# Order of the four weight sums, and the place of one quarter's parts, in the seven-product pairs of an output projection

## The chip, the core and the metric

The program runs on one core of one Trainium2 chip. The core has five engines with queues of their own that run at the same time and wait for each other through semaphores: TensorE (matmuls; PE in the profile, with its weight loads as PEld), VectorE (DVE), ScalarE (ACT), GpSimd (POOL) and SyncE (SP, which here only starts transfers). The metric is the device time of one execution in microseconds. Smaller is better.

## What is computed

Two layers of a decoder trunk, for 256 tokens of width 2048, all in float32. What matters of one layer:

```python
proj = rmsnorm(x) @ w_in[l]                       # 2048 -> 6144
q, k, v, gate_b, gate_c, conv_in = split(proj)    # 1024 columns each
attn = diff_attention(q, k, v)                    # 8 heads
conv = gate_b * short_conv(gate_c * conv_in)
x = x + concatenate([attn, conv]) @ w_out[l]      # the out-projection, 2048 -> 2048
x = x + relu(rmsnorm(x) @ w_up[l])**2 @ w_down[l] # 2048 -> 8192 -> 2048
```

## The kernel before

**Parts.** Each float32 operand of a matmul is held as two float32r tiles: hi, the rounded value (a ScalarE copy), and lo, the rest (a VectorE subtraction of hi from the value). A product is three matmuls: hi x hi, hi x lo, lo x hi. A weight thus comes as a load into a raw tile (started by SP), a copy on ScalarE and a subtraction on VectorE, and then TensorE can use it. A "split" or "rounding" below is this pair; the VectorE half is the last of it.

**Stages.** In each layer: q, k, v and the convolution's inputs; then the out-projection, whose left half (output columns 0 to 1023, `BySeven.left`, L939) is interleaved with the eight columns of the gate B projection; then its right half (`BySeven.right`, L1012); then the MLP.

**Sevens.** The out-projection goes over eight pairs i of 256 rows of w_out. Over a half of the output columns a pair is a 2 x 2 product of blocks. A "seven" makes it with seven products in place of eight (the scheme of Strassen and Winograd), for which sums of the blocks are needed: of the activations S1 to S4 (`sums_of`, L805), of the weights four sums in a tile t (`sums`, L854). With b11, b21 the left blocks and b12, b22 the right blocks of the weights, t[0] = b12 - b11, t[1] = b22 - b12, t[2] = t[1] + b11, t[3] = b21 - t[2]. The left half has five sevens (pairs 0 to 4, called a0 to a4 here for their first part and b0 to b4 for the second) and the right half two (pairs 2 and 3); the other pairs go the ordinary way, as chunks such as (0,5), which is output chunk 0 of pair 5. Two layers make fourteen sevens.

**The jobs of one seven** (`jobs`, L824), in the order in which they are taken:

- `plain` loads the left and the right raw tile (L842), splits b11 and b21 into the room w7b (pool tag "b"), and splits b22 into a tile whi and a tile wlo of wpool. All splits of this class have the lines L829 (ScalarE) and L830 (VectorE).
- `sums` forms t[0] (L859) and t[1] (L860), splits both into the room w7x, and forms t[2] (L864) and t[3] (L865).
- `more` splits t[2] and t[3] into the room w7y. w7x and w7y are the two buffers of biasp.

TensorE uses them in `product` (L881, matmuls at L884): first b11, b21, b22 (with S4) and t[0]; after another gate column t[1], then t[2] and t[3].

**Gate columns.** `column` (L948) makes one gate column out of two jobs with 128 columns of w_in each (splits at L326 and L327 by `halves`, L320; matmuls at L417), into one PSUM bank that all columns but the first share. `gate` (L771) then evicts the bank by ScalarE (L774), and VectorE forms y (L775, L776) and its parts (cat, L778 and L779). The next column can begin when the bank has been evicted. `LEFT` (L39) is the order, written out by hand: columns 0 and 1, a0, column 2, b0, column 3, a1, column 4, b1, column 5, a2, column 6, b2, column 7, a3, b3, the chunks (0,5) and (1,5), a4, b4, and the last chunks.

**Buffers.** All raw tiles of the stage share four buffers (`RAW`), so a load waits until the last reader of a raw tile is done. Each tile hi and each tile lo of the ordinary weights comes from wpool, with three buffers of each, also b22's. Jobs are made three ahead of their use (`take`, L381; `AHEAD`). The buffer "ao" of the pool tmp is a single one, 128 partitions by two times 512 float32; attention uses it (L650), and so does `results` (L905), which joins the seven products at the end of a half.

**What sets the order.** Only TensorE's instructions keep the order of the program text (`manual_schedule`), and single instructions that are marked `late`. Those of the other engines are ordered when the program is built, by a schedule on estimated times (`schedule_with_timeline_sim=True`). Each engine then works through its list in that order and waits at the first instruction that isn't ready.

Of the kernel before, what the change touches and what calls it, by code (L numbers as in the profile page):

```python
# [10 lines left out]
F32R = mybir.dt.float32r  # L11
# [4 lines left out]
P = 128  # L16
# [12 lines left out]
CH = 512  # L29
# [97 lines left out]
def trunk(ctx: ExitStack, tc: tile.TileContext, x, w_in, w_out, conv_w, q_norm_g, k_norm_g,  # L127
          lambda_q1, lambda_k1, lambda_q2, lambda_k2, subln_g, attn_norm_g, mlp_norm_g,
          w_up, w_down, rel_bias, selector, out):
    nc = tc.nc  # L130
# [4 lines left out]
    wpool = ctx.enter_context(tc.tile_pool(name="wpool", bufs=3))  # L135
# [650 lines left out]
    class BySeven:  # L786
# [37 lines left out]
        def jobs(self, w, i, col):  # L824

            mine = {}

            def split(hi, lo, src):
                nc.scalar.activation(hi, src, AF.Copy)  # L829
                nc.vector.tensor_sub(lo, src, hi.bitcast(F32))  # L830
                return hi, lo

            def two(room, src):

                hi, lo = split(room[:, 0], room[:, 1], src)
                return [(hi[:, j], lo[:, j]) for j in range(2)]

            def plain():
                raws = []
                for n in range(2):  # L840
                    raw = self.weights.pool.tile([P, 2, CH], F32, tag="raw", name="raw", bufs=RAW)
                    nc.sync.dma_start(  # L842
                        raw, w[2 * P * i:2 * P * (i + 1),
                               col + n * CH:col + (n + 1) * CH].rearrange(
                            "(k p) c -> p k c", p=P))
                    raws.append(raw)
                mine["raw"] = raws
                room = self.pool.tile([P, 2, 2, CH], F32R, tag="b", name="w7b")
                b11, b21 = two(room, raws[0])
                hi = wpool.tile([P, 2, CH], F32R, tag="hi", name="whi")  # L850
                lo = wpool.tile([P, 2, CH], F32R, tag="lo", name="wlo")
                return b11, b21, split(hi[:, 0], lo[:, 0], raws[1][:, 1])

            def sums():  # L854
                left, right = mine["raw"]
                pool, tag = (self.pool, "b") if col else (self.kpool, "kL")
                t = mine["t"] = pool.tile([P, 4, CH], F32, tag=tag, name="w7t")

                nc.vector.tensor_sub(t[:, 0], right[:, 0], left[:, 0])  # L859
                nc.vector.tensor_sub(t[:, 1], right[:, 1], right[:, 0])  # L860
                room = self.biasp.tile([P, 2, 2, CH], F32R, tag="bias", name="w7x")
                made = two(room, t[:, 0:2])

                nc.vector.tensor_add(t[:, 2], t[:, 1], left[:, 0])  # L864
                nc.vector.tensor_sub(t[:, 3], left[:, 1], t[:, 2])  # L865
                return made

            def more():
                room = self.biasp.tile([P, 2, 2, CH], F32R, tag="bias", name="w7y")
                return two(room, mine["t"][:, 2:4])  # L870

            return [plain, sums, more]

        def form(self, i, pa, a):
# [734 lines left out]
```

## Time and profile before

| what | us |
|---|---|
| median of three runs | 2130.81 |
| lowest and highest of them | 2129.49, 2132.07 |
| the profiled execution, its own time | 2129.56 |
| its span, from the first to the last instruction | 2127.8 |
| the left half of the out-projection in the first layer (from some 265 to 344 us), the gate columns ahead of it from 254 us | about 90 |
| the same in the second layer (from some 1323 to 1402 us), the gate columns from 1312 us | about 90 |

A row of a timeline reads: start, duration, engine, line, operation, tile written <- tiles read, partitions x elements and type, how many in a row. In square brackets stands how long the engine was idle before it and what ended that. A row of the waits reads: engine, its tile and line, <- the engine, tile and line it waited for: microseconds in all, times, the longest. A window's row reads: the stretch, its length, and then the busy time of TensorE, of its weight loads, of VectorE, of ScalarE and of GpSimd, each with its number of instructions, the granted clock of TensorE, the busy share of the DMA engines and the rate in GB/s.

### The profile page before, as it was taken

The numbers are of one execution on the slowest core, as the hardware profiler recorded it, in microseconds if no ns is written. First come the engines' busy times: TensorE is split into PE (matmuls) and PEld (weight loads), VectorE is DVE, ScalarE is ACT, GpSimd is POOL, SyncE is SP. The second block draws the span as 40 slices with busy tenths as digits, with TensorE's granted clock in tenths as the row PEclk, the third lists the DMA queues.
The fourth block names the chain that finished last, engine by engine and source line by source line (L and its number), as shares of the span: only waits on it lengthen the run. The fifth ranks groups of instructions, "written<-read, shape, count | busy, mean of one in ns | idle before, by whom it ended". The sixth has DMA issues, their size and how long they took to land.

```text
span 2127.8 us, 29379 instructions
## 1 busy us (share of the span) xinstructions
PE 2114.4 (99%) x10827; PEld 1805.0 (85%) x10827; DVE 1783.4 (84%) x2518; ACT 1402.2 (66%) x1880; POOL 171.3 (8%) x226
## 2 busy tenths in 40 slices
PE   9999999999999999999999999999999999999999
PEld 7888888888888888888888888788888888888887
DVE  6678788898888888799766787888988888888997
ACT  6777555677777777666566765556777777675664
POOL 3110110000000000011101102000000000000110
PEclk9999999999999999999999999999999999999999
DMA  8555565877777777788656555558877777777993
GB/s 271 178 158 178 170 197 189 288 252 226 230 234 231 234 232 230 248 303 289 216 169 181 164 169 178 172 194 292 259 234 232 230 230 234 233 232 256 318 312 103
DMA packets 314128, 476.02 MB, mean 224 GB/s; under 512 B 12707, under 2 KB 210165, under 8 KB 313984
## 3 DMA queue, kind: packets, MB, share of 16 engines
q1 hardware_dynamic: 285504, 406.76, 60.6%
q0 software_dynamic: 28288, 67.24, 10.0%
q8 instruction: 85, 1.39, 0.3%
q14 instruction: 59, 0.48, 0.1%
q10 hardware_dynamic: 192, 0.15, 0.0%
HBM read 440.52 MB, written 33.58 MB: 223 GB/s over the span
## 4 chain that ended last, share of the span: by engine, by line
PE 92%; DVE 3%; DMA 2%; ACT 1%; issue 1%; DVEq 0%; ACTq 0%; SPq 0%
PE upc L1296 31%; PE pr L1339 14%; PE dn L1420 8%; PE gc L465 4%; PE k L440 4%; PE q L440 4%; PE ci L465 4%; PE v L440 4%; PE o L898 3%; PE dn L1502 2%; DMA raw<-in_w_out_dram 2%; PE dn L1339 2%; PE po L898 2%; PE pr1r L1339 2%; PE pr0r L1339 1%; DVE wlo L327 1%
## 5 line engine op out<-in xcount | busy, mean ns | idle before, releaser
L1296 PE MATMUL upc<-nT,uhi 128*128 128x512 f32 x1920 | 454.7, 389 | 0.0
L1296 PEld LDWEIGHTS upc<-nT,uhi 128*128 128x128 f32 x1920 | 360.2, 188 | 74.7
L1160 DVE TENSOR_TENSOR ulo<-uraw,uhi 128x1024 fp32r<-128x1024 f32 x256 | 312.0, 1222 | 110.8 <-ACT f L1328 90.9
L327 DVE TENSOR_TENSOR wlo<-raw,whi 128x1024 fp32r<-128x1024 f32 x246 | 298.3, 1222 | 121.0 <-ACT whi L326 85.9
L326 ACT ACTIVATE whi<-raw 128x1024 fp32r<-128x1024 f32 x246 | 260.0, 1059 | 206.9 <-PE v L440 22.1
L1159 ACT ACTIVATE uhi<-uraw 128x1024 fp32r<-128x1024 f32 x256 | 270.7, 1057 | 159.1 <-PE upc L1296 139.2
L1296 PEld LDWEIGHTS upc<-nT,ulo 128*128 128x128 f32 x1920 | 246.2, 191 | 9.3
L1296 PE MATMUL upc<-nT,ulo 128*128 128x256 f32 x1920 | 249.1, 283 | 0.0
L1420 PE MATMUL dn<-whi,fb 128*128 128x512 f32 x496 | 156.7, 389 | 0.0
L1185 ACT ACTIVATE b2h<-draw 128x1024 fp32r<-128x1024 f32 x83 | 88.1, 1062 | 48.4 <-PE pr L1339 41.3
L326 ACT ACTIVATE whi<-uraw 128x1024 fp32r<-128x1024 f32 x62 | 65.9, 1063 | 81.7 <-PE dn L1420 62.8
L1420 PEld LDWEIGHTS dn<-whi,fb 128*128 128x128 f32 x496 | 93.1, 188 | 19.3
L1306 ACT ACTIVATE ev<-upc 128x512 f32<-128x512 f32 x120 | 72.0, 600 | 53.2 <-PE upc L1296 53.2
L1185 ACT ACTIVATE t24h<-t 128x1024 fp32r<-128x1024 f32 x83 | 88.2, 1063 | 22.5 <-PE pr L1339 15.9
L1186 DVE TENSOR_TENSOR t24l<-t,t24h 128x1024 fp32r<-128x1024 f32 x83 | 101.2, 1220 | 1.6
L1186 DVE TENSOR_TENSOR b2l<-draw,b2h 128x1024 fp32r<-128x1024 f32 x83 | 101.1, 1218 | 1.1 <-ACT b2h L1185 1.1
L1186 DVE TENSOR_TENSOR t13l<-t,t13h 128x1024 fp32r<-128x1024 f32 x83 | 101.2, 1219 | 0.8
L1199 DVE TENSOR_TENSOR t<-draw 128x1024 f32<-128x1024 f32 x83 | 101.2, 1220 | 0.3
L1185 ACT ACTIVATE t13h<-t 128x1024 fp32r<-128x1024 f32 x83 | 88.4, 1065 | 13.6 <-DVE t L1199 2.9
L1420 PE MATMUL dn<-wlo,fb 128*128 128x512 f32 x248 | 96.5, 389 | 0.0
L1339 PE MATMUL pr<-t13h,f 128*128 128x512 f32 x240 | 93.8, 391 | 0.0
L327 DVE TENSOR_TENSOR wlo<-uraw,whi 128x1024 fp32r<-128x1024 f32 x62 | 75.8, 1223 | 17.8 <-ACT whi L326 17.4
(486 smaller groups left out, 4441.0 us busy)
## 6 DMA issues: line engine op xcount, KB each, us to landing
uraw<-in_w_up_dram SPq DMA_DIRECT2D x128, 1024.0 KB, 6.3
raw<-in_w_in_dram SPq DMA_DIRECT2D x191, 512.0 KB, 4.1
draw<-in_w_down_dram SPq DMA_DIRECT2D x174, 512.0 KB, 5.3
raw<-in_w_out_dram SPq DMA_DIRECT2D x64, 512.0 KB, 4.5
uraw<-in_w_down_dram SPq DMA_DIRECT2D x62, 512.0 KB, 5.7
raw<-in_w_down_dram SPq DMA_DIRECT2D x10, 1024.0 KB, 5.4
hid0p<-f POOLq DMA_DIRECT2D x19, 512.0 KB, 3.5
fb<-hid0p POOLq DMA_DIRECT2D x19, 512.0 KB, 7.4
```

The lines of the kernel that those rows point to most:

```text
L326: pair = (nc.scalar.activation(hi, raw, AF.Copy), nc.vector.tensor_sub(lo, raw, hi.bitcast(F32)))
L327: nc.vector.tensor_sub(lo, raw, hi.bitcast(F32)))
L440: nc.tensor.matmul(acc[:, t], a.ap[:, pa, k % KG, t * P:(t + 1) * P], (hi, lo)[pw][:, j], start=(k == 0 and (pa, pw) == (0, 0)), stop=(k = ...
L465: nc.tensor.matmul(acc[:, f, 0] if part else acc[:, f], wt[:, k % 4, fs], a.ap[:, 0, k % KG] if part else a.ap[:, :, k % KG], start=(part ...
L898: nc.tensor.matmul(accs[t], a.ap[:, pa, k % KG, t * P:(t + 1) * P], (hi, lo)[pw][:, j], start=(j == 0 and m == 0 and (n, t) in starts), st ...
L1159: pair = (nc.scalar.activation(hi, src, AF.Copy), nc.vector.tensor_sub(lo, src, hi.bitcast(F32)))
L1160: nc.vector.tensor_sub(lo, src, hi.bitcast(F32)))
L1185: keep(nc.scalar.activation(hi, src, AF.Copy))
L1186: keep(nc.vector.tensor_sub(lo, src, hi.bitcast(F32)))
L1296: nc.tensor.matmul(acc[:, 0] if part else acc, wt[part][:, k], a.ap[:, 0, k % KG] if part else a.ap[:, :, k % KG], start=(part == 0 and kh ...
L1339: nc.tensor.matmul(prods[n], f[:, pa, a], b[pw], start=(start and m == 0), stop=(stop and m == 2))
L1420: nc.tensor.matmul(prods[p], f[:, pa, 2 * k + t], b[pw][:, n], start=(p in starts and k == 0 and m == 0), stop=(stop and k == 1 and m == 2))
```

## The change

In `plain`, the parts of b22 are no longer written into a tile hi and a tile lo of wpool, but into the two halves of a room w7c, which takes the single buffer "ao" of tmp. In `sums`, t[2] and t[3] are formed directly behind t[0] and t[1], ahead of the split of t[0] and t[1] in the program's text. No other line changes, and what is computed stays the same.

```diff
                 mine["raw"] = raws
                 room = self.pool.tile([P, 2, 2, CH], F32R, tag="b", name="w7b")
                 b11, b21 = two(room, raws[0])
-                hi = wpool.tile([P, 2, CH], F32R, tag="hi", name="whi")
-                lo = wpool.tile([P, 2, CH], F32R, tag="lo", name="wlo")
-                return b11, b21, split(hi[:, 0], lo[:, 0], raws[1][:, 1])
+                room = self.tmp.tile([P, 2, CH], F32R, tag="ao", name="w7c", bufs=1)
+                return b11, b21, split(room[:, 0], room[:, 1], raws[1][:, 1])
...
                 nc.vector.tensor_sub(t[:, 0], right[:, 0], left[:, 0])
                 nc.vector.tensor_sub(t[:, 1], right[:, 1], right[:, 0])
+                nc.vector.tensor_add(t[:, 2], t[:, 1], left[:, 0])
+                nc.vector.tensor_sub(t[:, 3], left[:, 1], t[:, 2])
                 room = self.biasp.tile([P, 2, 2, CH], F32R, tag="bias", name="w7x")
                 made = two(room, t[:, 0:2])

-                nc.vector.tensor_add(t[:, 2], t[:, 1], left[:, 0])
-                nc.vector.tensor_sub(t[:, 3], left[:, 1], t[:, 2])
                 return made
```

## The prediction

> **What bounds the kernel now.** I read the page's head first, then what TensorE waited for in the whole run, then the windows of the out-projection in both layers, and only then the queues of ScalarE and VectorE around each wait.
>
> ```profile
> span 2127.8 us, 29379 instructions
> PE 2114.4 (99%) x10827; PEld 1805.0 (85%) x10827; DVE 1783.4 (84%) x2518; ACT 1402.2 (66%) x1880; POOL 171.3 (8%) x226
> ```
> ```profile
> PE gb L417 <- ACT gb L774: 3.2, 4, 0.9
> PE po L884 <- DVE w7b L830: 2.6, 2, 1.3
> PE po L898 <- DVE wlo L327: 1.8, 2, 1.1
> ```
> ```profile
> 250.00:323.00 73.00, 69.40 (x370) 59.01 (x368) 60.73 (x87) 42.53 (x55) 7.09 (x1) 1.00 0.60 181
> 323.00:402.00 79.00, 79.00 (x380) 66.17 (x381) 67.48 (x95) 45.21 (x69) 0.89 (x2) 1.00 0.72 236
> 1308.00:1381.00 73.00, 68.96 (x367) 58.63 (x366) 60.08 (x86) 42.53 (x55) 7.10 (x1) 1.00 0.60 180
> 1381.00:1459.00 78.00, 78.00 (x376) 65.29 (x376) 66.90 (x94) 44.35 (x67) 0.89 (x2) 1.00 0.71 233
> ```
>
> TensorE is busy for 99% of the span, so no edit on VectorE or ScalarE gains by its own work; it gains what TensorE now waits. The three groups of waits add up to 3.2 + 2.6 + 1.8 = 7.6 us. All lie in the left half of the out-projection: its windows (first and third row; the columns are stretch, length, busy TensorE, weight loads, VectorE, ScalarE, GpSimd, clock, DMA) lack 73.00 - 69.40 = 3.60 and 73.00 - 68.96 = 4.04 us, together 7.64. The right half (second and fourth row) lacks nothing. That is the ceiling: 7.64 us, 0.36% of the run. The granted clock is 1.00 throughout.
>
> Here are the four waits in the first layer; the second has the same four.
>
> ```profile
> 269.07 3.92 PE L417 MATMUL gb<-nT,whi 128*128 128x512 f32 x16 [0.65 <-ACT gb L774]
> 286.24 3.94 PE L417 MATMUL gb<-nT,whi 128*128 128x512 f32 x16 [0.92 <-ACT gb L774]
> 301.19 1.43 PE L884 MATMUL po<-w7b,cat 128*128 128x512 f32 x5 [1.26 <-DVE w7b L830]
> 322.91 0.50 PE L898 MATMUL po<-wlo,cat 128*128 128x512 f32 x1 [0.77 <-DVE wlo L327]
> ```
>
> They stand before gate column 2, before column 4, inside seven a2 and at the first ordinary chunk (0,5). But TensorE is not what brings the stage to a2. In the chain of waits, the stretch before a2 is VectorE's queue and the loads:
>
> ```profile
> 270.18 4.88 DMA raw<-in_w_out_dram
> 285.57 5.42 DMA raw<-in_w_out_dram
> 299.92 1.23 DVE w7b L830
> 301.16 5.47 DMA raw<-in_w_out_dram
> 313.48 5.68 DMA raw<-in_w_out_dram
> ```
>
> So a wait that goes at column 2 or 4 only lets TensorE reach a2 sooner; it is a gain only as far as a2's rounding (L830, ended 301.15) also comes sooner. The sum hangs on this.
>
> **The sums moved ahead (L864, L865).** No instruction is added or removed: still two differences, two sums and two roundings a seven, fourteen sevens in all. The sums now precede the split of t1/t3. What does that free? In ScalarE's queue ahead of columns 2 and 4:
>
> ```profile
> 266.53 1.06 ACT L326 ACTIVATE whi<-raw 128x1024 fp32r<-128x1024 f32 x1 [2.25 <-DVE w7t L865]
> 267.50 1.04 ACT L829 ACTIVATE w7y<-w7t 128x1024 fp32r<-128x1024 f32 x1
> 268.45 0.57 ACT L774 ACTIVATE gb<-gb 128x512 f32<-128x512 f32 x1
> ```
> ```profile
> 282.87 1.06 ACT L326 ACTIVATE whi<-raw 128x1024 fp32r<-128x1024 f32 x1 [2.88 <-DMA raw<-in_w_in_dram]
> 283.83 1.04 ACT L829 ACTIVATE w7y<-w7t 128x1024 fp32r<-128x1024 f32 x1
> ```
>
> The eviction of column 1 (L774), for which TensorE waits, stands behind w7y, and w7y needs L865. ScalarE sat idle for 2.25 and 2.88 us just before. With L865 done earlier, w7y (its next instruction starts 0.95 later) fits into that idle time, and the eviction comes 0.95 sooner: more than the 0.65 and about the 0.92 that TensorE waits. I take both gate waits as gone from their places: 3.2 us in both layers, passed on to a2.
>
> What the move costs: w7x's rounding now stands behind L865.
>
> ```profile
> 280.91 1.22 DVE L830 TENSOR_TENSOR w7x<-w7t,w7x 128x1024 fp32r<-128x1024 f32 x1
> 284.48 0.84 PE L884 MATMUL po<-w7x,sf 128*128 128x512 f32 x3
> ```
>
> In a1 it would end 0.6 later than at 282.13, and TensorE needs it at 284.48, so 2.3 us of slack hide it; without that cover each seven would cost 0.6. The sums also become neighbours of what they read:
>
> ```profile
> 376.82 0.68 DVE L914 TENSOR_TENSOR e<-po0r,es 128x512 f32<-128x512 f32 x1
> 377.54 0.69 DVE L915 TENSOR_TENSOR es<-po0r,e 128x512 f32<-128x512 f32 x1
> 378.14 0.68 DVE L916 TENSOR_TENSOR x<-po0r,x 128x512 f32<-128x512 f32 x1
> ```
>
> L915 reads what L914 has just written and starts 0.72 after it; L916 does not read L915 and starts 0.60 after it. A direct dependence thus costs 0.12. Two per seven is 0.24. Two sevens (a1, a2) lie on VectorE's path to a2's rounding, in two layers: 4 x 0.24 = 1.0 us if the pairs stand directly together, 0 if other work falls between. I take 1.0. [...]
>
> **The right lower quarter in its own room.** The ring of three hi/lo tiles (wpool) loses one taker per seven, so a column's split after a seven waits for a matmul one tile further back. The new room is the single "ao" buffer, which attention and `results` also use. Its waits are on the product S4 x b22 of the seven before and on `results`' last sum: long done when the next b22 is formed. In a2 this copy starts at 291.09, a1's product S4 x b22 at 283.80. I cost it at nothing; for the right half, ScalarE today waits for the same product through the ring anyway.
>
> ```profile
> 291.09 0.63 ACT L829 ACTIVATE whi<-raw 128x512 fp32r<-128x512 f32 x1 [1.23 <-DMA raw<-in_w_out_dram]
> 283.80 0.39 PE L884 MATMUL po<-whi,sf 128*128 128x512 f32 x1
> ```
>
> Where the ring decides now: the split of chunk (0,5).
>
> ```profile
> 319.29 0.69 DVE L859 TENSOR_TENSOR w7t<-raw 128x512 f32<-128x512 f32 x1 [2.89 <-DMA raw<-in_w_out_dram]
> 321.64 2.35 DVE L327 TENSOR_TENSOR wlo<-raw,whi 128x1024 fp32r<-128x1024 f32 x2
> 314.52 1.04 ACT L326 ACTIVATE whi<-raw 128x1024 fp32r<-128x1024 f32 x1
> 315.05 2.08 PE L417 MATMUL gb<-nT,wlo 128*128 128x256 f32 x16
> ```
>
> Its hi was formed at 314.52, but its lo tile is the one that column 7 reads from 315.05 on; so its rounding was listed behind L859 of a4, which sat 2.89 us on its load, and TensorE stalled at 322.91. With one taker fewer its lo tile is one that column 6 has long left, and the rounding fits into the 2.89. I take this wait as gone: 1.8 us in both layers, with nothing late behind it, since what follows is paced by TensorE's own releases (the full second window).
>
> **What a2's rounding gains.** Two things move it. Column 4's first split waited for the ring (its row below); freed, it no longer stands right ahead of the second half's rounding, whose hi ended at 283.93 and which began at 283.18 + 1.14 = 284.3: about 0.35 sooner, and with it the load at 285.57. And the rounding at 292.56, of column 5, can go into the 1.59 that VectorE idles before L859, as its hi waited for TensorE, which now comes about 1.6 earlier: 1.14 (half of the 2.35 for two, less the overlap).
>
> ```profile
> 278.92 1.07 ACT L326 ACTIVATE whi<-raw 128x1024 fp32r<-128x1024 f32 x1 [1.32 <-PE gb L417]
> 291.01 0.69 DVE L859 TENSOR_TENSOR w7t<-raw 128x512 f32<-128x512 f32 x1 [1.59 <-DMA raw<-in_w_out_dram]
> 292.56 1.22 DVE L327 TENSOR_TENSOR wlo<-raw,whi 128x1024 fp32r<-128x1024 f32 x1
> ```
>
> Together 1.5 a layer. TensorE comes 1.6 sooner and waited 1.3 there already, so 1.3 + 1.6 - 1.5 = 1.4 of waiting is left a layer, 2.8 in both. The bounds: 0 if neither moves (2.9 left a layer), over 2.9 if all comes early (nothing left), and below nothing, -1.1, if w7y's rounding is now listed ahead of column 4's second half.
>
> **The sum:** 7.64 - 2.8 - 1.0 = 3.9 us gained (0.18%), with bounds of 7.64 - 2 x 4.0 - 1.0 = -1.4 and 7.6. The profiled execution took 2129.56 us (its span and 1.8 around it), so 2125.7 on its own scale. The median of the three runs is 1.25 above it; I forecast against the median: 2130.81 - 3.9 = **2126.9 us**.
>
> **The rivals.**
>
> *All four waits go* (0.19). The new free tile lets roundings run ahead and the loads behind them start sooner; at a2 only 1.5 more a layer is needed. For it: VectorE is busy for 60.73 of 73.00 in the window, so it has room. Against it: the loads' four buffers stay, and each lands 4.9 to 5.7 us after its issue. It gives 2130.81 - 7.6 = 2123.2. [...]
>
> *The change does not do what it says* (0.13). VectorE's queue does not follow the program's text; in a2 the sums already stand ahead of w7x's rounding:
>
> ```profile
> 295.23 0.69 DVE L865 TENSOR_TENSOR w7t<-raw,w7t 128x512 f32<-128x512 f32 x1
> 295.84 1.22 DVE L830 TENSOR_TENSOR w7x<-w7t,w7x 128x1024 fp32r<-128x1024 f32 x1
> ```
>
> If the queues come out as they are but for (0,5), 1.8 - 1.0 = 0.8 is gained: 2130.0.
>
> *Slower: one rounding more falls behind L859's load* (0.30). VectorE takes its list in order, and a rounding listed behind L859 waits for the load, as the two at 321.64 do. The re-listing can put a further 1.14 us there. TensorE has no slack at a2 and at a4, so from the first such rounding it counts in full: two places, two layers, 4 x 1.14 = 4.6, with the 1.0 of dependences 5.6: 2136.4. For it: every queue is listed anew, on estimated times, and the lists of before already hold places (2.89 at 319.29) where VectorE waits for a load with a ready rounding behind it. Against it: the change only frees tiles sooner.
>
> **How the numbers follow.** A measurement of this kernel can tell about 0.2% (4.3 us) from no change. The forecast's case (0.38) reaches from 2124.9 to 2128.9; somewhat under half of it lies beyond 0.2%. Faster: 0.19 + 0.18 = 0.37. Slower: 0.27 of the 0.30. Same: 0.20 + 0.13 + 0.03 = 0.36. The range leaves out the upper half of the slower case and the very end of the full gain: 2122.5 to 2136.8; the likeliest case's own range is the one above.
>
> **What would show it.** Right: no wait of TensorE on L774; w7y ahead of column 2's second split in ScalarE's queue; (0,5)'s rounding ahead of a4's L859; a wait of about 1.4 a layer left at a2; the left windows lacking about 3 instead of 7.6. Wrong: waits at new places in the left half, L859 idle longer than now, the load of a2's right side starting later relative to column 4, or any loss in the right half or in the MLP, which I take as unchanged because TensorE is full there.

## The result, and the profile after

| | median, us | lowest to highest | runs |
|---|---|---|---|
| before | 2130.15 | 2128.87 to 2132.07 | 4 |
| after | 2141.62 | 2140.74 to 2142.47 | 4 |

The changed kernel takes 1.0053 times as long (95% interval 1.0036 to 1.0070), 11.5 us more. The forecast was 2126.9, that is faster, with a range up to 2136.8: the time lies above that range. The profiled execution took 2142.22 us. In the changed kernel, line numbers behind the edit are smaller by one (product L883, pair L897), and the four sums are L858 to L861.

The head of the page of after:

```profile
span 2140.4 us, 29381 instructions
PE 2119.6 (99%) x10827; PEld 1808.5 (84%) x10827; DVE 1785.2 (83%) x2518; ACT 1402.2 (66%) x1880; POOL 165.6 (8%) x226
```

The work is the same, as many instructions as before on each engine, but TensorE is busy for 5.2 us more (2114.4 before), and the span is 12.6 longer (2127.8 before). The other part is in what TensorE waited for:

```profile
PE gb L417 <- ACT gb L774: 6.8, 5, 2.6
PE po L883 <- DVE w7b L830: 4.4, 2, 2.7
PE po L883 <- ACT w7b L829: 2.9, 2, 1.9
...
PE po1r L883 <- DVE w7y L830: 0.9, 1, 0.9
...
PE po0r L883 <- DVE w7y L830: 0.2, 1, 0.2
```

6.8 + 4.4 + 2.9 + 0.9 + 0.2 = 15.2 us, where the three groups of before made 7.6. So 7.6 us more of waiting and 5.2 more of busy time make 12.8, about the 12.6 of the span. The group of the chunk (0,5) is gone. The gate group has doubled, and a2 now waits for w7b's copy on ScalarE as well as for its rounding on VectorE. The windows, left and right half of both layers, show the place and something new (the eighth figure, the granted clock):

```profile
250.00:328.00 78.00, 71.17 (x370) 60.27 (x369) 66.15 (x93) 44.56 (x57) 4.49 (x1) 0.98 0.63 188
328.00:410.00 82.00, 81.83 (x395) 68.27 (x394) 65.49 (x92) 46.79 (x72) 0.89 (x2) 1.00 0.68 222
1310.00:1392.00 82.00, 74.73 (x383) 63.45 (x382) 68.38 (x98) 45.42 (x59) 4.48 (x1) 0.96 0.60 178
1392.00:1475.00 83.00, 82.02 (x392) 68.13 (x392) 65.46 (x91) 46.60 (x71) 0.89 (x2) 1.00 0.66 219
```

The left halves lack 6.83 and 7.27 us instead of 3.60 and 4.04, and their clock is no longer 1.00 but 0.98 and 0.96. The right halves, which lacked nothing, lack 0.17 and 0.98. TensorE's timeline of after, first layer and then second, has the waits of the left half one by one:

```profile
268.67 3.94 PE L417 MATMUL gb<-nT,whi 128*128 128x512 f32 x16 [0.82 <-ACT gb L774]
...
293.44 3.93 PE L417 MATMUL gb<-nT,whi 128*128 128x512 f32 x16 [0.95 <-ACT gb L774]
...
301.21 0.50 PE L883 MATMUL po<-w7b,cat 128*128 128x512 f32 x1 [1.94 <-ACT w7b L829]
303.44 2.50 PE L883 MATMUL po<-w7b,cat 128*128 128x512 f32 x5 [1.72 <-DVE w7b L830]
...
316.75 3.92 PE L417 MATMUL gb<-nT,whi 128*128 128x512 f32 x16 [1.39 <-ACT gb L774]
...
1333.34 5.54 PE L417 MATMUL gb<-nT,whi 128*128 128x512 f32 x16 [2.64 <-ACT gb L774]
...
1365.27 0.50 PE L883 MATMUL po<-w7b,cat 128*128 128x512 f32 x1 [0.98 <-ACT w7b L829]
...
1368.45 2.50 PE L883 MATMUL po<-w7b,cat 128*128 128x512 f32 x5 [2.68 <-DVE w7b L830]
1370.75 1.29 PE L883 MATMUL po<-w7c,sf 128*128 128x512 f32 x3
...
1381.36 3.92 PE L417 MATMUL gb<-nT,whi 128*128 128x512 f32 x16 [0.97 <-ACT gb L774]
```

They stand before columns 2, 5 and 7 and in a2 in the first layer, and before columns 2 and 7 and in a2 in the second.

Sixteen matmuls of a column, which take 3.94 us in the first row, take 5.54 behind the wait of 2.64; five of w7b take 2.50 behind the waits in a2, and 1.43 in before. Those are 1.6 and twice 1.07 of the 5.2 us of busy time, and the three of w7c behind them (1.29 instead of the usual 0.84) add some 0.45 a layer: 4.7 together. So a wait can cost more than itself: in these places the granted clock was lower around or behind the wait, 0.77 from 1332 to 1336 us, 0.66 from 304 to 308 and 0.57 from 1368 to 1372.

**Who makes TensorE wait.** This is ScalarE's timeline of after ahead of column 2, from the eviction of column 0 to that of column 1:

```profile
263.22 0.57 ACT L774 ACTIVATE gb<-gb 128x512 f32<-128x512 f32 x1
264.63 1.06 ACT L326 ACTIVATE whi<-raw 128x1024 fp32r<-128x1024 f32 x1 [0.83 <-DMA raw<-in_w_in_dram]
267.07 1.06 ACT L326 ACTIVATE whi<-raw 128x1024 fp32r<-128x1024 f32 x1 [1.38 <-DMA raw<-in_w_in_dram]
268.04 0.58 ACT L774 ACTIVATE gb<-gb 128x512 f32<-128x512 f32 x1
268.51 1.05 ACT L829 ACTIVATE w7y<-w7t 128x1024 fp32r<-128x1024 f32 x1
```

The eviction for which TensorE waits no longer stands behind w7y, which is now its next instruction. It stands behind a split whose load hadn't landed. Its load starts at 261.85, as the third behind a0's two, so it is column 3's first half, which TensorE needs only at 276.43. The chain of waits of after goes through this load, this split and this eviction.

And ahead of a2's w7b, ScalarE in after and then in before:

```profile
296.17 1.06 ACT L326 ACTIVATE whi<-raw 128x1024 fp32r<-128x1024 f32 x1 [1.84 <-DMA raw<-in_w_in_dram]
297.75 1.06 ACT L829 ACTIVATE w7y<-w7t 128x1024 fp32r<-128x1024 f32 x1 [0.52 <-DVE w7t L861]
298.85 1.06 ACT L326 ACTIVATE whi<-raw 128x1024 fp32r<-128x1024 f32 x1
...
300.12 1.04 ACT L829 ACTIVATE w7b<-raw 128x1024 fp32r<-128x1024 f32 x1
```

```profile
296.04 1.07 ACT L829 ACTIVATE w7y<-w7t 128x1024 fp32r<-128x1024 f32 x1 [2.15 <-PE gb L417]
297.01 1.04 ACT L326 ACTIVATE whi<-raw 128x1024 fp32r<-128x1024 f32 x1
...
298.26 1.05 ACT L829 ACTIVATE w7b<-raw 128x1024 fp32r<-128x1024 f32 x1
```

The list of after has one split more at its head, and it waits 1.84 us for a load; w7b begins 1.86 later, and TensorE's new wait there is 1.94.

The wait before column 7 has another copy ahead of it. This is ScalarE of after up to the eviction of column 6:

```profile
314.21 1.06 ACT L829 ACTIVATE w7b<-raw 128x1024 fp32r<-128x1024 f32 x1 [3.50 <-DMA raw<-in_w_out_dram]
...
316.12 0.58 ACT L774 ACTIVATE gb<-gb 128x512 f32<-128x512 f32 x1
```

The copy that waits 3.50 us for its load is not a column's split but w7b of a4. In before it stands behind this eviction (317.91 against 309.56). The second layer of after has the same, with 2.21 us.

**A count that shows the cause.** In each kernel's ScalarE timeline I counted the column splits (L326) between the w7b of a0 and each of the eight gate evictions. Both layers give the same numbers:

| kernel | splits listed ahead of eviction 0, 1, 2, ... 7 |
|---|---|
| before | 1, 3, 5, 7, 9, 11, 13, 15 |
| after | 2, 4, 6, 8, 10, 12, 14, 16 |

**Theory.** The ring of three hi tiles held the splits back. With b22's hi out of it, the schedule lists every column split one place further ahead. Some of these splits have loads that haven't landed when ScalarE comes to them: ahead of column 2 one waits 1.38 us (and once a layer it is w7b of a4 that is listed so early, with 3.50 in the first). ScalarE works in order, as in the rows above, where the eviction (268.04) comes only behind that split; so the evictions and w7b behind them come late, TensorE waits (0.82 us there), and behind some of the waits it runs slower for a while (5.54 us instead of 3.94 for sixteen matmuls). **Rivals:** the moved sums do it; the room's single buffer itself does, since it must be free before the next b22 is formed.

### The profile page after: what moved, and what is told of

The parts are those of the page before. It is cut to its first block, busy times and chain, and to the rows that moved or that the text cites. A ratio compares the mean times of both kernels' runs of the same rounds, so it can differ in the third digit from the quotient of the medians.

```text
span 2140.4 us, 29381 instructions
## 1 busy us (share of the span) xinstructions
PE 2119.6 (99%) x10827; PEld 1808.5 (84%) x10827; DVE 1785.2 (83%) x2518; ACT 1402.2 (66%) x1880; POOL 165.6 (8%) x226
## 4 chain that ended last, share of the span: by engine, by line
PE 93%; DMA 3%; DVE 2%; ACT 1%; issue 1%; SPq 0%; DVEq 0%; ACTq 0%
PE upc L1295 31%; PE pr L1338 13%; PE dn L1419 8%; PE gc L465 4%; PE k L440 4%; PE ci L465 4%; PE q L440 4%; PE v L440 4%; PE gb L417 2%; PE dn L1501 2%; PE dn L1338 2%; PE o L897 2%; PE po L883 2%; PE pr1r L1338 2%; DMA raw<-in_w_out_dram 1%; PE po L897 1%
## 5 line engine op out<-in xcount | busy, mean ns | idle before, releaser
L326 ACT ACTIVATE whi<-raw 128x1024 fp32r<-128x1024 f32 x246 | 260.1, 1059 | 229.5 <-issue 24.9
L326 ACT ACTIVATE whi<-uraw 128x1024 fp32r<-128x1024 f32 x62 | 65.9, 1062 | 81.8 <-PE dn L1419 62.6
```

Source lines behind the costliest of these rows:

```text
L326: pair = (nc.scalar.activation(hi, raw, AF.Copy), nc.vector.tensor_sub(lo, raw, hi.bitcast(F32)))
```

## The experiments

All times are medians; "before" is the kernel before on the same chip. "Waits" are TensorE's.

**One half of the change at a time.** First the new order of the sums with b22 in the ring as before, then the room with the sums as before.

```diff
# e1_sums_only, against after
-                room = self.tmp.tile([P, 2, CH], F32R, tag="ao", name="w7c", bufs=1)
-                return b11, b21, split(room[:, 0], room[:, 1], raws[1][:, 1])
+                hi = wpool.tile([P, 2, CH], F32R, tag="hi", name="whi")
+                lo = wpool.tile([P, 2, CH], F32R, tag="lo", name="wlo")
+                return b11, b21, split(hi[:, 0], lo[:, 0], raws[1][:, 1])
# e2_room_only, against before: the same lines the other way round
```

> Only the order of the sums is changed; b22's parts stay in the ring of three hi/lo tiles. If the freed places of the ring do the harm (theory), the splits stay where they were in ScalarE's queue: 2127 to 2133 us, TensorE's waits 6 to 9 us, no drop of the clock. If the sums do the harm (rival), most of the 11 us is here: 2138 to 2144 us.

> Only b22's parts move to the single room; the sums stay behind the split of t1 and t3. If the freed places of the ring do the harm (theory), nearly all of it is here: 2138 to 2146 us, with a split two columns ahead listed before an eviction, TensorE's waits of 12 us or more, and slow matmuls after the longest of them. If the sums do it (rival): 2128 to 2133 us.

Measured: the sums alone 2130.50 against 2129.74 (ratio 1.0002, 0.9992 to 1.0011); the room alone 2139.09, that is 9.35 us more (1.0041, 1.0026 to 1.0056). The waits of the sums alone:

```profile
PE po L898 <- DVE wlo L327: 3.7, 2, 2.3
PE gb L417 <- ACT gb L774: 3.2, 4, 0.9
PE po L884 <- DVE w7b L830: 2.7, 2, 1.3
```

The wait of (0,5) has grown from 1.8 to 3.7 us, without a loss in time that can be told. The room alone has the groups of after: 5.8 us for evictions, 3.8 for w7b on ScalarE and 3.5 on VectorE.

With the sums moved, the gate waits are what they were, to the tenth. VectorE's timeline of that kernel says why:

```profile
280.10 1.22 DVE L830 TENSOR_TENSOR w7x<-w7t,w7x 128x1024 fp32r<-128x1024 f32 x1
281.23 0.69 DVE L862 TENSOR_TENSOR w7t<-raw,w7t 128x512 f32<-128x512 f32 x1
```

In a1, around the second gate wait, the last sum (t[3], L862 there) still stands behind w7x's rounding, as in before: the schedule didn't follow the text. It is so in a0 too. The count of splits is that of before (1, 3, 5, ...) for the sums and that of after (2, 4, 6, ...) for the room. So the room carries nearly all of the loss, and the sums by themselves carry none that can be told.

**Which half of the room.** Only one part of b22 goes into the room, the other stays in the ring.

```diff
# e8_lo_in_room, against before
                 hi = wpool.tile([P, 2, CH], F32R, tag="hi", name="whi")
-                lo = wpool.tile([P, 2, CH], F32R, tag="lo", name="wlo")
-                return b11, b21, split(hi[:, 0], lo[:, 0], raws[1][:, 1])
+                room = self.tmp.tile([P, 2, CH], F32R, tag="ao", name="w7c", bufs=1)
+                return b11, b21, split(hi[:, 0], room[:, 1], raws[1][:, 1])
# e9_hi_in_room: the other way round, split(room[:, 0], lo[:, 0], ...)
```

> The kernel before, with only the lo part of b22 in the single room; its hi part stays in the ring, and no queueing is forced. The room's own wait (on the product of the seven before) is as in the change, but ScalarE finds no free hi place more than before. If the freed hi places do the harm (theory): 2127 to 2134 us. If the single room's wait does (rival): 2136 us or more.

> The reverse: the hi part of b22 in the single room, its lo part in the ring. ScalarE has the freed hi places and can copy ahead. If the freed hi places do the harm (theory): 2135 to 2142 us, near the room alone. If it takes both or the lo places: 2128 to 2133 us.

Measured: lo in the room 2128.01 against 2129.69 (0.9990, 0.9981 to 0.9999); hi in the room 2137.09 (1.0033, 1.0020 to 1.0046), 7.4 us more. Count of splits: 1, 3, 5, ... with lo there; 2, 4, 6, ... with hi there (only the last is 15). The waits with lo in the room:

```profile
PE po L884 <- DVE w7b L830: 2.5, 2, 1.2
PE po L884 <- ACT w7b L829: 1.2, 2, 1.0
```

and with hi:

```profile
PE gb L417 <- ACT gb L774: 8.7, 6, 3.4
PE po L884 <- DVE w7y L830: 2.7, 2, 1.4
...
PE po L884 <- DVE w7b L830: 0.8, 1, 0.8
```

The hi part does the harm, as the theory says, since only hi places let ScalarE's copies go ahead. The lo part is the useful half, by some 1.7 us: with it alone in the room the gate waits and that of (0,5) are both gone, as I had forecast of the whole. With hi alone in the room (0,5) doesn't wait either, but there the gate waits have grown.

**The place or the room?** With hi in the room, a ring place is free and a single buffer is in use, both at once. This run tells them apart: hi is formed twice, in its ring place and in the room, and TensorE reads both.

```diff
# e13_place_kept, against before
-                return b11, b21, split(hi[:, 0], lo[:, 0], raws[1][:, 1])
+                room = self.tmp.tile([P, 2, CH], F32R, tag="ao", name="w7c", bufs=1)
+                nc.scalar.activation(room[:, 0], raws[1][:, 1], AF.Copy)
+                return b11, b21, (*split(hi[:, 0], lo[:, 0], raws[1][:, 1]), room[:, 0])
...
-                nc.tensor.matmul(self.prods[n], self.form(i, pa, a), b[pw],
+                part = b[2] if m == 0 and len(b) > 2 else b[pw]
+                nc.tensor.matmul(self.prods[n], self.form(i, pa, a), part,
```

> The kernel before, with one copy more a seven: the hi part of b22 is formed twice, in its place in the ring as before and in the single buffer ao; TensorE reads the copy in ao for hi x hi and the one in the ring for lo x hi. So the ring keeps its taker and the room's single buffer is in use as in the changed kernel. Theory (the place that comes free in the ring lets one column split be listed ahead of an eviction): with the place taken again, ScalarE has 1, 3, 5, 7 column splits between the w7b of a0 and the first, second, third, fourth eviction, as before, not 2, 4, 6, 8; the 14 copies more take 0.63 us each on ScalarE, which is idle for a third of the run; 2129 to 2133 us. Rival (the single buffer itself holds up ScalarE or TensorE, as it must be free before the next hi is formed): most of the 7.4 us that hi in the room alone cost stays, 2135 to 2140 us, at whatever count of splits.

Measured: 2130.47 against 2129.06 (1.0001, 0.9992 to 1.0010), and the count is 1, 3, 5, ... again. Its waits:

```profile
PE gb L417 <- ACT gb L774: 3.1, 4, 1.3
PE po L887 <- DVE w7b L830: 2.7, 2, 1.3
PE po L901 <- DVE wlo L327: 2.6, 2, 1.3
```

These are the groups of before. With the ring's place taken again, no loss can be told although the room is used by every seven: it is the free place, not the room, that costs. What stays open: in this run ScalarE never waits for TensorE at the extra copy in the left half, but in after it does so twice in each layer, at a3 and a4 (first layer):

```profile
ACT w7c L829 <- PE po L883: 2.2, 2, 1.5
```

They come after the waits at columns 2 and 5 and in a2, and so can't be the cause of those. Column 7's wait comes behind the one at a3. There the load that w7b of a4 waits for starts at 309.40, when VectorE has rounded a3's w7c. But VectorE comes to that rounding only at 308.69, straight from the last sum, while ScalarE's copy, which had waited 0.78 us, was done at 307.77. So by these rows the room's own wait isn't what delays that load. A second buffer for the room was not tried, so what these waits cost isn't measured by itself.

**Taking the order in hand.** If splits ahead of evictions do the harm, listing them behind must take it away. Each column split is listed behind the last gate eviction that the program has reached; in after and in before.

```diff
# e4_after_pinned against after, e5_before_pinned against before
+    evicted = []
+
     def gate(c, acc, cv, dst, y):
...
-        nc.scalar.activation(ev, acc, AF.Copy)
+        evicted.append(nc.scalar.activation(ev, acc, AF.Copy))
...
-                    return self.halves(raw)
+                    if not evicted:
+                        return self.halves(raw)
+                    with tc.issue_after(evicted[-1].ins):
+                        return self.halves(raw)
...
+            evicted.clear()
             by_seven.left(hT, cv)
```

> The changed kernel, with each gate column's split queued on ScalarE behind the last gate eviction that the program text has ahead of it. If the evictions and a2's copy of b11 and b21 are late because splits that still wait for a load stand ahead of them (theory), TensorE's waits on L774 fall from 6.8 to under 2 us and the time to 2126 to 2135 us. If the single room's own wait on the product of the seven before does it (rival), the time stays at 2138 us or more.

> The kernel before with the same queueing of the splits behind the evictions. Theory: the waits of 3.2 us on L774 go, but the load and VectorE chain to a2 stays, so a2's wait grows by a part of it: 2126 to 2131 us. If evictions are no part of it: the same time as before within 1 us, with the waits on L774 unchanged.

Measured: after with this order 2130.29 against 2129.74 (0.9999, 0.9989 to 1.0008), so the loss of the change is gone; before with it 2123.47 (0.9970, 0.9958 to 0.9982), 6.3 us faster than before. The count ahead of the second eviction falls to 2 in both. In after so ordered the waits for evictions fall to 1.8 us, as expected; those for w7b stay, 2.3 on VectorE and 1.9 on ScalarE. For before I had expected the reverse of what came: the waits for evictions to go and a2's to grow. One group is left:

```profile
PE gb L420 <- ACT gb L779: 3.2, 4, 1.2
```

These waits are as long as before but stand at columns 3 and 5, and those in a2 and at (0,5) are gone. In the first layer w7b's rounding for a2 now starts at 297.02 with a column's rounding behind it (298.16); in before it stood behind one (298.78 and then 299.92).

**The two halves of the change again, in that order of the list.** The room, and the moved sums, each put into the kernel before so ordered (e5 below, as the labels are shortened from here on).

```diff
# e6_pinned_room: e5 and the room (as e2); e7_pinned_sums: e5 and the moved sums (as e1)
```

> Queueing behind the evictions and the room, the sums as before. The queueing alone gave 2123.5 us, with the room and the moved sums 2130.3. If it is the room that costs the difference even in the pinned queue: 2128 to 2132 us, with a2 still waiting for w7b. If it is the moved sums: 2122 to 2126 us.

> Columns' splits queued behind the evictions, the sums moved ahead, b22 in the ring as before. The queueing alone gave 2123.5 us, with the room 2130.2, with both 2130.3. If the sums cost nothing (theory): 2121 to 2126 us. If they cost as much as the room: 2128 us or more.

Measured: with the room 2130.17 against 2129.69 (1.0000, 0.9991 to 1.0010), so the room costs 6.7 us against e5 here too (on another chip, where before took the same within 0.1 us); with the sums 2123.72 against 2129.14 (0.9974, 0.9964 to 0.9984), 0.25 from e5 and not to be told from it. The counts of both runs and of e5 are the same up to the sixth eviction (1, 2, 5, 6, 9, 10). So evictions behind early splits are only one way in which the free place costs. In the room's run TensorE waits 2.6 us for evictions, 2.3 + 2.2 for w7b (on VectorE and on ScalarE) and 0.8 for w7y on the right; in e5 only the 3.2 for evictions.

**The sevens' copies too.** The ScalarE copies of the left half's sevens are also listed behind the last eviction: in before, in after, and in before with lo of b22 in the room.

```diff
# e10_all_pinned (against e5), e11_after_all_pinned (against e4), e12_all_pinned_lo_room (e10 and e8)
             def split(hi, lo, src):
-                nc.scalar.activation(hi, src, AF.Copy)
+                copy = nc.scalar.activation
+                if self.evicted and not col:
+                    with tc.issue_after(self.evicted[-1].ins):
+                        copy(hi, src, AF.Copy)
+                else:
+                    copy(hi, src, AF.Copy)
```

> The kernel before, with the columns' splits and also the sevens' copies in the left half queued behind the last eviction ahead of them in the text. The columns' splits alone left 3.2 us of waits on L774, behind a copy of b22 that waits for its load. If that copy is the cause: these waits fall under 1 us and the time to 2119 to 2123 us. If the copies are then too late for a1 and a2: new waits on w7b, 2124 us or more.

> The changed kernel with the columns' splits and the sevens' copies queued behind the evictions. If all that the room costs comes through ScalarE's order around evictions: 2119 to 2124 us, as the kernel before does with that queue. If VectorE's order ahead of a2's w7b costs too, as the pinned room's 2130.2 suggests: 2125 to 2131 us, with a wait of a2 on w7b and none on L774.

> The kernel before with all copies queued behind the evictions, and only the lo part of b22 in the single room. Queueing alone gave 2121.7 us and lo in the room alone 1.7 us less than before. If the two gains add: 2118 to 2121 us. If they take away the same waits: 2120 to 2123 us.

Measured: before so ordered 2121.68 against 2129.69 (0.9963, 0.9949 to 0.9977); after so ordered 2127.41 against 2129.14 (0.9989, 0.9980 to 0.9999); with lo in the room 2121.17 against 2129.14 (0.9961, 0.9946 to 0.9975). The first and the last beat both kernels: that of before by some 8 us, that of after by some 20. The 0.5 us between the two can't be told from nothing, so the gains of the order and of lo in the room don't add. What still parts after from before when both are so ordered, some 6 us, can be read in part on VectorE ahead of a2. After so ordered:

```profile
295.32 1.22 DVE L327 TENSOR_TENSOR wlo<-raw,whi 128x1024 fp32r<-128x1024 f32 x1
...
296.79 1.22 DVE L840 TENSOR_TENSOR w7b<-raw,w7b 128x1024 fp32r<-128x1024 f32 x1
```

before so ordered:

```profile
296.16 1.23 DVE L840 TENSOR_TENSOR w7b<-raw,w7b 128x1024 fp32r<-128x1024 f32 x1
297.30 1.22 DVE L327 TENSOR_TENSOR wlo<-raw,whi 128x1024 fp32r<-128x1024 f32 x1
```

With the free place, a column's rounding stands ahead of w7b's; without it, behind. TensorE then waits 1.52 us for w7b's rounding in after so ordered, and 0.35 in before so ordered. With the second layer a2 waits 3.6 us in the one and 1.3 in the other, a difference of 2.3. Another 1.8 is waiting for w7y on the right, which before so ordered doesn't have, and TensorE is busy for 3.1 us more (2114.2 and 2111.1). That VectorE's order is the rest of the room's cost is thus argued from these rows, and for a part of it; no run isolates it.

## Why the prediction was wrong, step by step

**"The right lower quarter in its own room": the step that failed.** I costed it at nothing, since only the room's own waits seemed able to cost. The room alone costs 9.35 us, hi alone 7.4, and nothing that can be told once the ring's place is taken again. I had even noted that a column's split then "waits for a matmul one tile further back", and booked that as relief. But a split that no longer waits for a tile is listed earlier, and there it waits for its load (1.38 us ahead of column 2), with an eviction behind it. That is not the whole: with the splits listed behind the evictions the room still costs 6.7 us, for which the orders ahead of a2's w7b and on the right are argued, not isolated. Nor was the product of the seven before always "long done": at a3 and a4 ScalarE waited for it, 2.2 us a layer, though no cost of that could be shown.

**The chunk (0,5)** was right: its wait of 1.8 us is gone in after, with its rounding (316.45) ahead of the first difference of a4 (320.86), and it is gone with lo alone in the room. With hi alone it is gone too, so the freed lo place isn't shown to be the only way; and the hi place took more than all this gave.

**"The sums moved ahead":** wrong by its whole 3.2 us. With the sums alone, both gate waits stay. In a0 and a1, t[3] doesn't move ahead of w7x's rounding in VectorE's list, so w7y can't come sooner. In after, w7y did leave its place ahead of column 1's eviction, but a split with an unlanded load took that place: a wait instead of a wait, 0.65 before and 0.82 now at column 2, and in the second layer 0.80 and 2.64.

**The 1.0 us of dependences** doesn't show. In e1 the first of the two last sums still has other work between it and the second, and e7 stands 0.25 us from e5. In after they stand together only in a3, off the path to a2: there t[3] starts 0.72 us after t[2] (307.36 and 308.08), and the next instruction 0.61 after that. So some 0.11 stands there, about the 0.12 that I had read, but not where I had counted it; no run prices it.

**"What a2's rounding gains":** forecast 1.5 a layer sooner, but in the first layer w7b's copy begins 1.86 later, and the rounding itself 2.24 later (302.16 instead of 299.92).

**The clock at 1.00 throughout, and the right half unchanged:** both wrong, 5.2 us of busy time and 1.1 of waiting (w7y, 0.9 + 0.2). On the right w7y's rounding stands behind the next seven's w7b in after (368.03 and then 369.17); in before it starts ahead of it. All runs with hi and lo in the room have this wait, those with one part there don't; no run isolates it.

**The slower rival** (0.30, 2136.4) had the mechanism, an in-order engine stuck at a load with ready work behind it, but on VectorE at L859 and by way of the re-listing; it was ScalarE at L326, by way of the free place. My reason against it, that "the change only frees tiles sooner", is the cause itself. (The sum of the forecast comes to 3.8 by its own terms, not 3.9, which changes nothing.) **That the change doesn't do what it says** held for the sums.

## What to carry to other kernels

Where a schedule made on estimated times fills in-order queues, a scarce buffer also sets how far ahead a helper engine may run. Before freeing a place, count how many look-ahead copies would then stand ahead of each instruction that the bounding engine waits for, and see whether their loads have landed. Move the part that helps (here lo, 1.7 us) and leave the part that holds the order (here hi), or list the look-ahead work behind the evictions by hand, which was worth 8 us here. A change in the program's text that the schedule is free to undo should be looked for in the list of the engine before it is priced.

## What the runs showed of the hardware that I had not expected

The granted clock fell around waits of under 3 us. In after, windows of 4 us (as above; the eighth figure is the clock) behind a2 in the first layer and around column 2 in the second:

```profile
304.00:308.00 4.00, 4.00 (x13) 3.20 (x12) 3.66 (x6) 1.36 (x3) 0.00 (x0) 0.66 0.64 225
1332.00:1336.00 4.00, 2.66 (x8) 2.13 (x9) 4.00 (x7) 2.23 (x3) 2.64 (x1) 0.77 0.78 256
```

It fell to 0.77 around one wait of 2.64 us, and to 0.66 behind two of 1.94 and 1.72 with 0.5 us of work between them. In the sums alone it was 1.00 behind one wait of 2.28:

```profile
1382.12 0.50 PE L898 MATMUL po<-wlo,cat 128*128 128x512 f32 x1 [2.28 <-DVE wlo L327]
```

The window behind it, in the same kernel:

```profile
1384.00:1388.00 4.00, 4.00 (x20) 3.28 (x19) 4.00 (x7) 2.31 (x3) 0.00 (x0) 1.00 0.88 272
```

Nor did the length alone decide in these runs. With the splits ordered by hand and the room (e6), a2 has two waits of 1.03 and 1.15 us in the first layer and two of 1.15 in the second, each pair with 0.5 us of work between:

```profile
300.44 2.50 PE L888 MATMUL po<-w7b,cat 128*128 128x512 f32 x5 [1.15 <-DVE w7b L835]
...
1360.09 1.42 PE L888 MATMUL po<-w7b,cat 128*128 128x512 f32 x5 [1.15 <-DVE w7b L835]
```

The five matmuls behind the first pair took 2.50 us, those behind the second 1.42. By the ratio of these two times, the clock behind the first pair is estimated at 0.57 of that behind the second.

In e6 nearly the same pair of waits thus came out both ways, and no run here shows what decides it. The mean granted clock of whole executions varied too: e5 and e12, whose longest waits in the out-projection were 1.2 and 0.8 us, and e10 had 1.000 in each of their 15 runs, which lie within 2.7 us for each of the three, and e7 had it in seven of eight; before has between 0.997 and 1.000, and its runs on one chip spread over 7.4 us.
